# Three wide products moved between the q and k groups of a mixer, and one convolution tap moved to ScalarE

## The chip, the cores and the metric

The kernel runs on one core of one Trainium2 chip. The metric is the device time of one execution in microseconds, smaller is better. Before the change it is 1267.02 us, the median of three runs (1266.68 to 1269.48).

## What is computed

A trunk of two layers over 256 tokens of 1024 channels, in float32. Each layer is a SwiGLU, a mixer and a SwiGLU again. The mixer multiplies the normed input once by `w_in` and cuts the columns into pieces for two branches:

```python
h = rmsnorm(x, norm_mix[l])
gq, gk, gv, gz, gb, ga, c_q, c_kv, k_rope, gate_logits = split_cols(h @ w_in[l])
y_a = gdn_branch(gq, gk, gv, gz, gb, ga, gdn_conv[l], ...)
y_b = mla_branch(c_q, c_kv, k_rope, cos, sin, ...)
gates = jax.nn.sigmoid(gate_logits).reshape(B, S, N_BRANCH, D)
x = x + (gates[:, :, 0] * y_a + gates[:, :, 1] * y_b) @ w_out[l]
```

The first branch is a gated delta rule in both directions: q, k and v (512 columns each) pass through a convolution of five taps along the tokens and a SiLU, the lengths of q and k are divided out, a triangular system is solved for each of four heads and each direction, and the result is normed and multiplied by silu(z). The second branch is attention of eight heads from low-rank latents.

## The kernel before

**Products.** A float32 matrix is multiplied as two float32r parts. `weights` (L111 to L127) loads a slice of a weight matrix into `raw` by the SyncE queue (L114), ScalarE rounds it to `whi` (L122), VectorE subtracts to get `wlo` (L123); `raw`, `whi` and `wlo` have three buffers each, a `whi` holds up to 1024 columns a partition. `dense_t` (L137) then runs three TensorE products per chunk of 128 input channels and per tile of 128 tokens: L133 (`xh` by `whi`), L134 (`xh` by `wlo`), L135 (`xl` by `whi`). A block of 512 columns over eight chunks has 48 such products and four pairs `whi`, `wlo`. The sums lie in the PSUM tiles `acc`, of which there are three.

**Groups of q, k, v.** `qkv_group` (L528) makes two of the twelve chunks of channels, channel-major: 48 products of 256 columns at L536 into one `acc`; the second chunk of channels takes the weights from the last to the first. VectorE multiplies by the norm into `pre` (L543) and runs the convolution: for each of the two chunks one tap at L549 and four at L551, all on VectorE, into `cv`. ScalarE does a tanh (L555), VectorE the product (L556). `pre` and `cv` have one buffer each. Groups 2 and 3 are k, 0 and 1 are q, 4 and 5 are v.

**Inversion.** `gdn_decay` (L712) makes decay tables on GpSimd (L721, L733); `gdn_la` (L736) forms the products L741 and the matrices `LA` (L745). `gdn_base` (L759) brings the 16-blocks of `LA` into place (VectorE L769, ScalarE L771, VectorE L774, L777, L778), inverts them on GpSimd in 30 small steps (L783, L785) and brings them back (VectorE L788, L790, ScalarE L793, VectorE L794). `inv0` to `inv5` build the whole inverse with many small TensorE products, the first of them at L817. `gdn_first`, `gdn_second` and `gdn_out` (L930, then VectorE L933, ScalarE L936, GpSimd L99, VectorE L947) follow, and L472 transposes the result.

**Attention.** `mla_dense` makes q, k, v of four heads (products with latents, ScalarE L603 and L607, VectorE L608, rotation on GpSimd L589 to L594), `mla_heads` transposes them (L629, copies L632 on ScalarE). A head is L642, VectorE L644, ScalarE L650, VectorE L652 and L654, transposes L659, a copy to SBUF (L664 or L666), L671.

**Order.** The calls are written out by hand at the end of `mixer` (L980 to L1053). The SyncE queue follows that order of calls. On the other engines the framework that builds the program sets the order of instructions ahead of time from these calls and its own timing; each engine then works through its list in that order and waits at the first instruction that isn't ready. The mixer runs twice.

Of the kernel before, what the change touches and what calls it, by code (L numbers as in the profile page):

```python
# [11 lines left out]
F32 = mybir.dt.float32  # L12
# [8 lines left out]
P = 128  # L21
# [16 lines left out]
def encoder_trunk(ctx: ExitStack, tc: tile.TileContext, x, positions, norm_ffn1, ffn1_w_gate, ffn1_w_up,  # L38
# [23 lines left out]
    # the tensor engine's clock rises while the first loads run  # L62
# [8 lines left out]
    # columns of gains: ffn1 (8 per layer), mix, ffn2, q latent (3), kv latent (2), gdn (1)  # L71
# [29 lines left out]
    def split(hi, lo, ps, gain=None):  # L101
        """hi + lo = gain * ps, both exact in float32r."""
        if gain is None:
            A.copy(out=hi, in_=ps)
            V.tensor_tensor(out=lo, in0=ps, in1=hi.bitcast(F32), op=ALU.subtract)
        else:
            A.activation(out=hi, in_=ps, func=AF.Copy, scale=gain)  # L107
            V.scalar_tensor_tensor(out=lo, in0=ps, scalar=gain, in1=hi.bitcast(F32), op0=ALU.mult,  # L108
                                   op1=ALU.subtract)

    def weights(src, nk, w, pool=wpool):  # L111
        """A [nk*128, w] slice of weights, as (hi, lo) tiles of up to 1024 elements a partition."""
# [16 lines left out]
    def mm3(ps, a, w, n, start, stop, ts=range(NT)):  # L129
        """ps[t] (+)= a^T w in three passes, for the token tiles ts."""  # L130
        for t in ts:
            a1, a2 = (v[:, t * P:(t + 1) * P] for v in a)
            T.matmul(ps[t][:, :n], lhsT=a1, rhs=w[0], start=start, stop=False)  # L133
            T.matmul(ps[t][:, :n], lhsT=a1, rhs=w[1], start=False, stop=False)  # L134
            T.matmul(ps[t][:, :n], lhsT=a2, rhs=w[0], start=False, stop=stop)  # L135

    def dense_t(acts, src, c0, w, evac, tail=4, pool=wpool):  # L137
        """evac(t, psum [128 tokens, w]) of acts @ src[:, c0:c0+w]; acts: (hi, lo) [128, tokens] of each chunk.
        The last chunks (tail or fewer) go through for one token tile, then for the other."""
# [22 lines left out]
    def dense_halves(acts, parts):  # L162
        """dense_t for two parts (src, c0, evac) of 512 columns: the first half of the chunks for both, then the second."""
# [11 lines left out]
    def to_chan(srcs, hi, lo, kc, gain0=None):  # L175
        """Transposes srcs[t] ([128 tokens, n*128]) into chunks kc.. of hi / lo [128, chunk, tokens]."""
# [22 lines left out]
    def x_done(t, cg):  # L199
        """Half cg of x's tile t is final: sum of squares."""  # L200
        A.activation(out=junk, in_=x_sb[:, t, cg * 512:(cg + 1) * 512], func=AF.Square,
                     accum_out=state["ss"][:, t, cg:cg + 1])
# [67 lines left out]
    def finale(down):  # L270
        """The last x, its norm, the result; x of the first half lies by its gains before the second is there."""
# [37 lines left out]
    def mixer_consts(tmp):  # L309
# [16 lines left out]
        alog = const.tile([P, depth, 8], F32, name="alog")  # -exp(A_log)  # L326
# [12 lines left out]
        # m[p, f]  # L339
# [6 lines left out]
        # half[:, 0]: partition % 32 < 16, half[:, 1]: the others  # L346
# [7 lines left out]
        # the off-diagonal 16-blocks of the 32-blocks on the diagonal: below it (mlo) and above it (mup)  # L354
# [11 lines left out]
        # rotary tables  # L366
# [42 lines left out]
    def mixer(l, next_gain):  # L409
# [7 lines left out]
        with tc.tile_pool(name="mix", bufs=1) as mp:  # L417
# [16 lines left out]
            def rstd_row():  # L434
                """rstd along the free axis, the same in every partition."""
# [26 lines left out]
            def to_chan2(srcs, gains):  # L462
                """Chunks of 128 channels, two to a tile: a list of (hi, lo) [128, tokens]."""
# [35 lines left out]
            def gdn_scalars():  # L499
# [4 lines left out]
                # softplus(a) = max(a, 0) + log1p(exp(-|a|))  # L504
# [14 lines left out]
            qkT = mp.tile([P, 8, S], F32, name="qkT")  # L519
            vT = {}  # lies in ysb until ysb is written  # L520
# [4 lines left out]
            def qkv_group(grp):  # L525
                """Two of the twelve chunks of channels."""
# [3 lines left out]
                # one group of sums after the other: they share a bank. The second takes the weights from the last on  # L530
# [13 lines left out]
                for c in range(2):  # L544
                    ch = grp * 2 + c
                    for d in range(5):
                        wc = ccol[:, l * 60 + d * 12 + ch:l * 60 + d * 12 + ch + 1]
                        if d == 0:
                            V.tensor_scalar(out=cv[:, c], in0=pre[:, c, 0:S], scalar1=wc, scalar2=None, op0=ALU.mult)  # L549
# [3 lines left out]
                # 2 silu(.); the lengths and |k| v below take account of the 2  # L553
# [5 lines left out]
            def lengths(c0):  # L559
                """1/|.| of four of the eight heads of q and k, a column for each head."""  # L560
                pss = gdp()[:, :4 * NT * 32].rearrange("p (c t s) -> p c t s", c=4, t=NT)
                for c in (0, 2):
# [3 lines left out]
                    for g in range(4):  # L566
                        # the sums for the tokens of group g, in each of its partitions
# [28 lines left out]
            def mla_dense(hf):  # L596
                """q, k, v of four heads, token-major, rotary parts turned."""
# [22 lines left out]
            def mla_heads(q, k, v):  # L620
                """attend(pair of heads), of the four that q, k, v hold."""
# [57 lines left out]
            LA, Z, egc, cs = {}, {}, {}, {}  # L679
            LAd = {}  # L680
            for d in range(2):
                LAd[d] = mp.tile([P, NT, NH, 2, P], F32, name=f"LA{d}")  # [.., 0, :] for q, [.., 1, :] for k
# [7 lines left out]
            def gdn_coeffs():  # L690
# [3 lines left out]
                # -beta / |k|^2  # L694
# [17 lines left out]
            def gdn_decay(t):  # L712
                """E[j, h, i]: decay from token j to token i of the tile, 0 where i comes before j."""
                for d in range(2):
# [10 lines left out]
                    if t == d:  # L725
                        # first tile of this direction: decay of each token up to the carried state
# [5 lines left out]
                    # hi_m[p, f] holds where f is at or after p in this direction  # L732
# [25 lines left out]
            def gdn_base():  # L758
                """XC, ZC: inverses (and transposes) of the 16-blocks on the diagonal, each block in a partition of its  # L759
                own meanwhile."""  # L760
# [47 lines left out]
            def inv_zero():  # L808
                """Z = X^T = (1 + L)^-T from the inverted 16-blocks: blocks of 32, 64, 128 in turn."""
                for d in range(2):  # L810
                    G.memset(Z[d], 0.0)
# [21 lines left out]
            def inv2(d):  # L833
# [9 lines left out]
                # the 64-block that the last step takes X from  # L843
# [41 lines left out]
            def gdn_first(d):  # L885
                """First tile of direction d: its solution, and what it adds to the other tile."""
# [39 lines left out]
            def gdn_out(t):  # L926
# [10 lines left out]
                # o here is -|q| sqrt(128) times the true one, zs_t is 2 silu(z) / rstd  # L937
# [43 lines left out]
            rstd_row()  # L981
            qkv_group(2)
            dense(xh, xl, NKC, wl_, C_BA, 400, ev_ba)
            qkv_group(3)
            qkv_group(0)
            dense(xh, xl, NKC, wl_, C_KV, 288, ev_kv)
            gdn_scalars()
            gdn_decay(0)
            lengths(4)
            cqT = latent(cq, QL, 0, G_Q + 3 * l)  # L990
            qkv_group(1)
            gdn_decay(1)
            ckT = latent(ckv, KVL, 2, G_KV + 2 * l)
            nk_ = gdn_coeffs()
# [5 lines left out]
            dense(xh, xl, NKC, wl_, C_Z, 512, ev_z)  # L1000
# [7 lines left out]
            gb = [gate(C_G + D)]  # L1008
            gb.append(gate(C_G + D + 512))
# [46 lines left out]
    new_norm()  # L1056
    state["squares"] = False  # of the input: once its products run
# [32 lines left out]
```

## Time and profile before

| What | Value |
| --- | --- |
| median of three runs | 1267.02 us |
| span of the profiled execution, first to last instruction | 1260.2 us |
| TensorE (PE) busy | 1230.4 us, 98% |
| VectorE (DVE) busy | 774.1 us, 61% |
| ScalarE (ACT) busy | 623.4 us, 49% |
| GpSimd (POOL) busy | 132.5 us, 11% |
| mean granted TensorE clock | 0.993 |

The profile gives the profiled execution by its span; the runs' times are taken from outside, and their median is 6.8 us above the span, which is what lies ahead of the first instruction and behind the last. The kernel is a queue of TensorE work with few gaps, so it is read by looking for the stretches in which TensorE is idle or runs at a lower clock, and for what ended each wait.

### The profile page before, as it was taken

Reading aid. Unit: us, or ns where it says so; the run is one execution under the profiler, and the core shown is the slowest. Engines: PE = TensorE matmul, PEld = TensorE weight load, DVE = VectorE, ACT = ScalarE, POOL = GpSimd, SP = SyncE. Lnnn points to the kernel's source line nnn. Section 1 sums busy time; section 2 is a strip of 40 time slices with the busy share of each in tenths; the row PEclk is TensorE's granted clock in tenths of the full one; section 3 lists DMA queues with packets and bytes.
Section 4 is the critical chain, followed back from the end, with each engine's and each line's share of the span. In section 5 each row is a group of like instructions: output and inputs, shape, how many; then the busy total and the mean of one; then the engine's idle time right before and its main releaser. Section 6 shows DMA issues by size and latency. Waiting matters only on the chain.

```text
span 1260.2 us, 17612 instructions
## 1 busy us (share of the span) xinstructions
PE 1230.4 (98%) x7064; PEld 1031.9 (82%) x7064; DVE 774.1 (61%) x1127; ACT 623.4 (49%) x911; POOL 132.5 (11%) x237
## 2 busy tenths in 40 slices
PE   9999999899999999999999999998999999999997
PEld 6888889777988788888888888897778787888886
DVE  5655556986757665554555554588876576555554
ACT  6554445546445455443445443465555455544443
POOL 1000001445001000000000000015540000000010
PEclk9999999999999999999999999999999999999999
DMA  7554554435222555555555555543442245565552
GB/s 266 175 197 153 198 184 157 153 119 167 71 99 95 164 176 181 187 169 198 182 187 182 185 167 201 177 147 123 150 162 74 68 134 184 168 199 179 188 184 84
DMA packets 114576, 202.70 MB, mean 161 GB/s; under 512 B 4107, under 2 KB 30399, under 8 KB 114495
## 3 DMA queue, kind: packets, MB, share of 16 engines
q1 hardware_dynamic: 114031, 200.52, 47.8%
q8 instruction: 55, 0.90, 0.3%
q10 hardware_dynamic: 464, 1.06, 0.2%
q14 instruction: 26, 0.21, 0.1%
HBM read 200.52 MB, written 1.05 MB: 160 GB/s over the span
## 4 chain that ended last, share of the span: by engine, by line
PE 88%; DVE 4%; POOL 4%; issue 1%; ACT 1%; DMA 0%; POOLq 0%; SPq 0%; ACTq 0%
PE acc L133 24%; PE acc L134 23%; PE acc L135 23%; PE acc L536 4%; PE ms L183 2%; DVE wlo L123 2%; POOL bt L783 1%; PE ms L671 1%; PE ms L642 1%; POOL t L785 1%; PE gd L134 1%; PE gd L135 1%; PE gd L133 1%; PE gd L912 1%; DVE cv L551 1%
## 5 line engine op out<-in xcount | busy, mean ns | idle before, releaser
L123 DVE TENSOR_TENSOR wlo<-raw,whi 128x1024 fp32r<-128x1024 f32 (+3 forms) x388 | 471.2, 1217 | 371.0 <-ACT whi L122 369.0
L122 ACT CAST whi<-raw 128x1024 fp32r<-128x1024 f32 (+3 forms) x388 | 398.8, 1031 | 435.9 <-PE acc L135 392.0
L134 PE MATMUL acc<-wlo,xh 128*128 128x512 f32 (+3 forms) x968 | 360.7, 374 | 0.0
L135 PE MATMUL acc<-whi,xl 128*128 128x512 f32 (+3 forms) x968 | 357.5, 372 | 0.0
L133 PE MATMUL acc<-whi,xh 128*128 128x512 f32 (+3 forms) x968 | 344.9, 376 | 0.1
L134 PEld LDWEIGHTS acc<-wlo,xh 128*128 128x128 f32 x968 | 182.4, 188 | 29.8 <-issue 0.4
L133 PEld LDWEIGHTS acc<-whi,xh 128*128 128x128 f32 x968 | 181.4, 188 | 30.4 <-ACT xh L107 0.8
L135 PEld LDWEIGHTS acc<-whi,xl 128*128 128x128 f32 x968 | 182.1, 188 | 29.3
L134 PE MATMUL acc<-wlo,hh 128*128 128x512 f32 x352 | 138.9, 395 | 0.0
L135 PE MATMUL acc<-whi,hl 128*128 128x512 f32 x352 | 138.7, 394 | 0.0
L133 PE MATMUL acc<-whi,hh 128*128 128x512 f32 x352 | 129.1, 397 | 0.0
L135 PEld LDWEIGHTS acc<-whi,hl 128*128 128x128 f32 x352 | 65.9, 187 | 16.1
L133 PEld LDWEIGHTS acc<-whi,hh 128*128 128x128 f32 x352 | 65.9, 187 | 15.9
L134 PEld LDWEIGHTS acc<-wlo,hh 128*128 128x128 f32 x352 | 65.9, 187 | 15.3
L133 PE MATMUL acc<-whi,fr 128*128 128x512 f32 (+1 forms) x152 | 60.9, 407 | 9.2 <-DVE pre L543 7.9
L134 PE MATMUL acc<-wlo,fr 128*128 128x512 f32 (+1 forms) x152 | 61.0, 404 | 0.0
L135 PE MATMUL acc<-whi,fr 128*128 128x512 f32 (+1 forms) x152 | 58.2, 400 | 2.3 <-DVE fr L108 2.3
L536 PE MATMUL acc<-xl,whi 128*128 128x256 f32 x192 | 55.6, 289 | 0.0
L536 PE MATMUL acc<-xh,whi 128*128 128x256 f32 x192 | 55.5, 291 | 0.0
L536 PE MATMUL acc<-xh,wlo 128*128 128x256 f32 x192 | 53.3, 288 | 0.0
L551 DVE SCALAR_TENSOR_TENSOR cv<-pre,ccol,cv 128x256 f32<-128x256 f32 x96 | 51.6, 569 | 0.0
L246 ACT ACTIVATE sil<-acc,rstd 128x512 f32<-128x512 f32 (+1 forms) x48 | 31.0, 654 | 29.5 <-PE acc L135 29.4
(298 smaller groups left out, 1273.3 us busy)
## 6 DMA issues: line engine op xcount, KB each, us to landing
raw<-in_ffn_w_up_dram SPq DMA_DIRECT2D x40, 1024.0 KB, 4.9
raw<-in_ffn_w_down_dram SPq DMA_DIRECT2D x40, 1024.0 KB, 4.9
raw<-in_ffn_w_gate_dram SPq DMA_DIRECT2D x38, 1024.0 KB, 4.9
raw<-in_w_in_dram SPq DMA_DIRECT2D x32, 1024.0 KB, 4.8
raw<-in_w_out_dram SPq DMA_DIRECT2D x8, 1024.0 KB, 4.8
raw<-in_ffn_w_gate_dram SPq DMA_DIRECT2D x12, 512.0 KB, 3.5
raw<-in_ffn_w_up_dram SPq DMA_DIRECT2D x8, 512.0 KB, 3.5
raw<-in_ffn_w_down_dram SPq DMA_DIRECT2D x8, 512.0 KB, 3.3
```

What stands on the lines that cost most here:

```text
L122: A.copy(out=hi[:, :n * w], in_=raw[:, k0 * w:(k0 + n) * w])
L123: V.tensor_tensor(out=lo[:, :n * w], in0=raw[:, k0 * w:(k0 + n) * w], in1=hi[:, :n * w].bitcast(F32), op=ALU.subtract)
L133: T.matmul(ps[t][:, :n], lhsT=a1, rhs=w[0], start=start, stop=False)
L134: T.matmul(ps[t][:, :n], lhsT=a1, rhs=w[1], start=False, stop=False)
L135: T.matmul(ps[t][:, :n], lhsT=a2, rhs=w[0], start=False, stop=stop)
L183: T.transpose(out=pt[:, i * S + t * P:i * S + (t + 1) * P], in_=srcs[t][:, (j + i) * P:(j + i + 1) * P], identity=ident)
L246: A.activation(out=sil[t][:, :w], in_=ps, func=AF.Silu, scale=rstds[0][:, t:t + 1])
L536: T.matmul(pc[:, c], lhsT=w[:, cc], rhs=a, start=(i == 0), stop=(i == len(terms) - 1))
L551: V.scalar_tensor_tensor(out=cv[:, c], in0=pre[:, c, d:d + S], scalar=wc, in1=cv[:, c], op0=ALU.mult, op1=ALU.add)
L642: T.matmul(sc[:, t * S:(t + 1) * S], lhsT=qT[:, t * P:(t + 1) * P], rhs=kT, start=True, stop=True)
L671: T.matmul(po[r:r + MV, :S], lhsT=v[:, kk, h, :], rhs=prT[:, kk, :], start=(kk == 0), stop=(kk == NT - 1))
L783: G.tensor_tensor(out=tv, in0=M[:, b + 1:16, b:b + 1].to_broadcast([P, na, nb]), in1=Y[:, b:b + 1, 0:nb].to_broadcast([P, na, nb]), op=ALU ...
```

## The change

Three blocks of 512 columns are called earlier, and nothing is removed. The two gate blocks of the second branch (`gb`) move from behind `mla_dense(1)` to between the groups: the first behind group 3, the second behind `lengths(4)`. The `kv` block moves ahead of group 0. The z block moves from behind `gdn_base` to behind the second latent. In the convolution the first tap of each chunk of channels (L549) becomes a ScalarE activation that copies with a scale. Comments and docstrings are blanked, so that line numbers below L979 stay.

```diff
@@ qkv_group @@
                         if d == 0:
-                            V.tensor_scalar(out=cv[:, c], in0=pre[:, c, 0:S], scalar1=wc, scalar2=None, op0=ALU.mult)
+                            A.activation(out=cv[:, c], in_=pre[:, c, 0:S], func=AF.Copy, scale=wc)
                         else:
...
@@ order of calls @@
             rstd_row()
+
             qkv_group(2)
             dense(xh, xl, NKC, wl_, C_BA, 400, ev_ba)
             qkv_group(3)
+            gb = [gate(C_G + D)]
+            dense(xh, xl, NKC, wl_, C_KV, 288, ev_kv)
             qkv_group(0)
-            dense(xh, xl, NKC, wl_, C_KV, 288, ev_kv)
             gdn_scalars()
             gdn_decay(0)
             lengths(4)
+            gb.append(gate(C_G + D + 512))
             cqT = latent(cq, QL, 0, G_Q + 3 * l)
             qkv_group(1)
             gdn_decay(1)
             ckT = latent(ckv, KVL, 2, G_KV + 2 * l)
+            dense(xh, xl, NKC, wl_, C_Z, 512, ev_z)
             nk_ = gdn_coeffs()
...
             gdn_base()
-            dense(xh, xl, NKC, wl_, C_Z, 512, ev_z)
             inv_zero()
...
             m1 = mla_dense(1)
-            gb = [gate(C_G + D)]
-            gb.append(gate(C_G + D + 512))
             inv3(0)
```

The first place is the SyncE queue in the first part of the mixer, from group 3 on. A load of 8x256 is a q, k or v group, 4x288 the kv block, 4x512 half of a gate or z block, and `mla_w_ukv`, `mla_w_uq` are for `mla_dense`. Before:

```order
L114 DMA raw_1832<-in_w_in_dram 128x8x256
L114 DMA raw_1909<-in_w_in_dram 128x8x256
L114 DMA raw_1987<-in_w_in_dram 128x4x288
L114 DMA raw_2021<-in_w_in_dram 128x4x288
L114 DMA raw_2143<-in_w_in_dram 128x8x256
L114 DMA raw_2299<-in_mla_w_ukv_dram 128x2x512
L114 DMA raw_2323<-in_mla_w_uq_dram 128x3x384
L114 DMA raw_2477<-in_w_in_dram 128x4x512
L114 DMA raw_2511<-in_w_in_dram 128x4x512
L114 DMA raw_2730<-in_mla_w_ukv_dram 128x2x512
L114 DMA raw_2754<-in_mla_w_uq_dram 128x3x384
L114 DMA raw_2796<-in_w_in_dram 128x4x512
```

After the change:

```order
L114 DMA raw_1832<-in_w_in_dram 128x8x256
L114 DMA raw_1912<-in_w_in_dram 128x4x512
L114 DMA raw_1946<-in_w_in_dram 128x4x512
L114 DMA raw_1984<-in_w_in_dram 128x4x288
L114 DMA raw_2018<-in_w_in_dram 128x4x288
L114 DMA raw_2057<-in_w_in_dram 128x8x256
L114 DMA raw_2197<-in_w_in_dram 128x4x512
L114 DMA raw_2231<-in_w_in_dram 128x4x512
L114 DMA raw_2291<-in_w_in_dram 128x8x256
L114 DMA raw_2409<-in_w_in_dram 128x4x512
L114 DMA raw_2443<-in_w_in_dram 128x4x512
L114 DMA raw_2523<-in_mla_w_ukv_dram 128x2x512
```

Groups 3, 0 and 1 stood next to each other but for the kv block; now a block of 512 columns stands behind each of them.

The second place is ScalarE where `gdn_base` begins; `LA0` and `tb` are the matrices of the two directions, `qk` the transposed q and k of the first four heads, `m3` and `whi_3147` belong to the second four heads and to the second half of the weights of group 4. Before, from the first copy at L771 on:

```order
L771 COPY g2_2397<-LA0_1657 32x8x2x16 x4
L650 ACTIVATE pr_2974,sm_2975<-ms_2968,mxs_2971 128x256 x2
L771 COPY g2_2397<-tb_2402 32x8x2x16
L122 CAST whi_2836<-raw_2830 128x1024
L122 CAST whi_2872<-raw_2870 128x1024
L771 COPY g2_2397<-tb_2405 32x8x2x16
L122 CAST whi_2876<-raw_2870 128x1024
L771 COPY g2_2397<-tb_2408 32x8x2x16
L963 ACTIVATE gate_2792<-acc_2794,hrstd_1632 128x512
L771 COPY g2_2397<-tb_2411 32x8x2x16
```

After:

```order
L771 COPY g2_2621<-tb_2626 32x8x2x16
L632 COPY qk_2596<-ms_2591 96x512
L632 COPY qk_2603<-ms_2598 96x512
L771 COPY g2_2621<-tb_2629 32x8x2x16
L632 COPY qk_2610<-ms_2605 96x512
L607 ACTIVATE m3_2874<-acc_2876,lrs_1643 128x4x64
L607 ACTIVATE m3_2874<-acc_2877,lrs_1643 128x4x64
L632 COPY qk_2617<-ms_2612 96x512
L603 ACTIVATE m3_2873<-acc_2900,lrs_1643 128x384
L771 COPY g2_2621<-tb_2632 32x8x2x16
L771 COPY g2_2621<-tb_2635 32x8x2x16
L122 CAST whi_3147<-raw_3141 128x1024
```

Casts of gate weights stood between the copies; now it is the copies and evacuations of attention, and the next cast stands behind the last copy.

The third place is TensorE at the end of the delta rule; `gd_3673` and `gd_3701` are its outputs for token tiles 0 and 1, `ms_3602` and `ms_3585` belong to the last head of attention. Before, the last products of L930 and what follows:

```order
L930 MATMUL gd_3701<-LA1_1661 128x128
L930 MATMUL gd_3701<-LA0_1657 128x128
L930 MATMUL gd_3701<-LA1_1661 128x128
L134 MATMUL acc_3731<-wlo_3770,xh_98 128x512
L135 MATMUL acc_3731<-whi_3769,xl_99 128x512
```

After:

```order
L671 MATMUL ms_3585<-pr_3583,mv_2875 64x256 x2
L642 MATMUL ms_3588<-qk_3342,qk_3335 128x256 x2
L930 MATMUL gd_3701<-LA1_1661 128x128
L930 MATMUL gd_3701<-LA0_1657 128x128
L930 MATMUL gd_3701<-LA1_1661 128x128
L659 MATMUL ms_3602<-ident_86,pr_3594 128x128
L472 MATMUL ms_3805<-ident_86,g2_3665 128x128
L659 MATMUL ms_3602<-ident_86,pr_3594 128x128 x3
L671 MATMUL ms_3585<-pr_3607,mv_2875 64x256 x2
L472 MATMUL ms_3814<-ident_86,g2_3665 128x128
```

Behind L930 stood 22 products of a gate block and twelve of 512 columns; now the last head of attention is there, and the transposes of the result stand next to it.

## Rows read from the trace of the kernel before

**Rows 1.** Busy time by stretch: first three of mixer one, then of mixer two.

```profile
core 0: us, PE busy (x) PEld busy (x) DVE busy (x) ACT busy (x) POOL busy (x), PEclk, DMA share, GB/s
198.30:282.10 83.80, 76.07 (x479) 69.40 (x478) 72.20 (x141) 46.27 (x81) 33.21 (x43) 0.96 0.44 142
282.10:317.70 35.60, 34.18 (x179) 28.12 (x179) 26.05 (x44) 24.02 (x40) 18.05 (x39) 1.00 0.45 148
317.70:395.30 77.60, 77.22 (x852) 65.80 (x851) 48.97 (x101) 35.01 (x71) 6.15 (x10) 0.98 0.22 73
822.10:903.90 81.80, 73.96 (x475) 67.42 (x474) 71.10 (x138) 46.25 (x81) 33.32 (x43) 0.98 0.44 144
903.90:940.40 36.50, 35.08 (x185) 28.90 (x184) 27.00 (x47) 24.04 (x40) 18.06 (x39) 1.00 0.46 148
940.40:1016.70 76.30, 75.93 (x851) 64.59 (x852) 48.95 (x101) 35.21 (x72) 6.13 (x10) 1.00 0.23 75
```

**Rows 2.** The same columns, for four short windows of mixer one.

```profile
232.00:252.00 20.00, 13.80 (x83) 12.02 (x82) 19.88 (x28) 9.61 (x21) 14.38 (x13) 0.91 0.44 152
252.00:256.00 4.00, 4.00 (x21) 3.65 (x20) 0.36 (x1) 1.64 (x3) 0.00 (x0) 0.59 0.00 0
312.00:316.00 4.00, 2.58 (x23) 2.41 (x22) 3.76 (x8) 1.48 (x3) 1.15 (x3) 1.00 0.00 0
324.00:332.00 8.00, 8.00 (x182) 7.74 (x180) 4.57 (x13) 2.15 (x7) 1.19 (x4) 0.79 0.01 2
```

**Rows 3.** What TensorE waited for: total us, times, longest.

```profile
PE acc L133 <- DVE pre L543: 7.9, 2, 3.9
```

**Rows 4.** VectorE in order of time: start us, us.

```profile
235.44 2.01 DVE L549 TENSOR_SCALAR cv<-pre,ccol 128x256 f32<-128x256 f32 x2
237.53 1.90 DVE L123 TENSOR_TENSOR wlo<-raw,whi 128x1024 fp32r<-128x1024 f32 x1
...
284.49 1.21 DVE L123 TENSOR_TENSOR wlo<-raw,whi 128x1024 fp32r<-128x1024 f32 x1
```

**Rows 5.** Two scalings of 128x256, tap and ScalarE: minimum, median, maximum in ns.

```profile
L549 DVE TENSOR_SCALAR cv<-pre,ccol x24: 342/347/1127, 209.6 to 958.9; 128x256 f32<-128x256 f32 x24
L107 ACT ACTIVATE xh<-ms,gcol x48: 454/474/502, 8.3 to 1072.5; 128x256 fp32r<-128x256 f32 x48
```

**Rows 6.** TensorE in order of time (two), and from the chain (one).

```profile
287.39 0.39 PE L135 MATMUL acc<-whi,xl 128*128 128x512 f32 x1
287.61 0.39 PE L133 MATMUL acc<-whi,xh 128*128 128x512 f32 x1
...
203.85 3.83 PE acc L536 x32
```

**Rows 7.** From LA to L817, each engine's own timeline, with its wait in brackets.

```profile
283.70 0.86 DVE L745 SCALAR_TENSOR_TENSOR LA<-gd,negc,g 128x256 f32<-128x256 f32 x2
284.84 2.70 ACT L771 COPY g<-LA 32x256 f32<-32x256 f32 x4
295.44 0.65 ACT L771 COPY g<-tb 32x256 f32<-32x256 f32 x1 [1.08 <-DVE tb L769]
297.89 1.19 POOL L783 TENSOR_TENSOR bt<-t,t 128x15 f32<-128x15 f32 x1 [8.67 <-DVE t L778]
312.17 1.18 DVE L788 TENSOR_SCALAR g<-t,half 128x256 f32<-128x256 f32 x2 [4.50 <-POOL t L785]
317.63 1.91 PE L817 MATMUL gd<-XC,LA 32*32 32x32 f32 x64
```

**Rows 8.** Copies of attention on ScalarE: minimum, median, maximum in ns.

```profile
L632 ACT COPY qk<-ms x16: 567/585/597, 273.2 to 969.5; 96x512 f32<-96x512 f32 x16
```

**Rows 9.** Around L930: TensorE, VectorE and TensorE in order of time.

```profile
383.41 1.08 PE L671 MATMUL ms<-pr,mv 128*64 128x256 f32 x4
392.03 3.51 PE L930 MATMUL gd<-LA 128*128 128x128 f32 x30
393.99 0.68 DVE L933 TENSOR_TENSOR g<-gd,g 128x512 f32<-128x512 f32 x1
398.72 1.14 DVE L947 SCALAR_TENSOR_TENSOR g<-g,fac,zsil 128x128 f32<-128x128 f32 x4
403.18 0.38 PE L472 MATMUL ms<-ident,g 128*128 128x128 f32 x2
```

## The prediction

> **What bounds the kernel now.** I read busy time by stretch first, because TensorE is 98% busy over the whole span and only its gaps can be won. I cut each mixer where its chain of work changes hands: stretch 1 from the first q, k product to the last L741, stretch 2 from there to the first L817, stretch 3 from there to the last L930, stretch 4 the rest. [rows 1] show them as span, then busy time: TensorE is idle 7.7 us of stretch 1 in mixer one (83.80 less 76.07) and 7.8 us in mixer two, 1.4 us of stretch 2 in both, 0.4 us of stretch 3 in both. The granted clock shows a second loss: 0.96 and 0.98 in stretch 1, 0.98 in stretch 3 of mixer one. The two levels are 1.2 and 2.4 GHz, so a mean below 1 is time at the lower one.
>
> Second, short windows of stretch 1 [rows 2]: from 232 to 252 us TensorE is busy 13.80 of 20 us while VectorE is busy 19.88. VectorE is the limit there, not TensorE. Right behind the hole the clock is 0.59 for 4 us. Third, the waits: the longest single one of TensorE is for `pre` at L543, 3.9 us in each mixer [rows 3]: the `acc` of group 1 is held until VectorE has evacuated it, and VectorE is still at the taps of group 0, since `pre` and `cv` have one buffer. Fourth, VectorE's timeline there [rows 4]: two first taps take 2.01 us and a subtraction 1.90 us, where one elsewhere takes 1.21; GpSimd is busy 14.38 us of the same window [rows 2], and I take that as the cause of the slowness.
>
> So in stretch 1 four groups ask VectorE for more than TensorE asks of itself, bunched. In stretches 2 and 3 it is the opposite: long serial chains of small steps (inversion, attention) that wide blocks cover.
>
> **The change part by part.** A block of 512 columns costs TensorE 48 products of 0.22 to 0.23 us (the distance of two starts [rows 6]), 11 us, and VectorE four subtractions of 1.21 [rows 4], 4.9 us. A group costs TensorE 48 times 0.12 us (3.83 us for 32 [rows 6]), 5.8 us.
>
> *Stretch 1.* It gains two gate blocks, 22 us of TensorE. The z block was in it before already. The second four heads of `mla_dense` and the transposes L629 and L642 leave it for stretch 2, 8.1 us. TensorE's work is 76.1 less some 2.8 us lost to the clock, plus 22 less 8.1: 87 us. VectorE's load is 72.2 us [rows 1], plus 9.8 for the gates, less 3.3 that leaves with the heads, less the first taps: eight at 0.35 us by the median, at 1.1 us the slowest [rows 5]; I take 0.52, 4.2 us. That makes 74.5 of 87 us, 86%, the same share as before, but now each group's taps have 11 us of TensorE work beside them. The `acc` of a group is needed again only by the second block behind it. Hence the wait of [rows 3] goes. What is late next are `wlo` of the gate blocks, which stand between taps, with three buffers. I take 1.5 us of idle time for each mixer; bounds 0.5 (nothing late) and 4 (half of the present hole). Gain: 15.6 less 3.0 us idle in both mixers, and the clock: (1 less 0.96) of 83.8 is 3.4, of which some 0.9 fell into the hole and cost nothing, and 1.6 in mixer two, 4.2 together. **Stretch 1: 16.8 us faster** over both mixers.
>
> *The tap on ScalarE.* ScalarE is busy 46 of 84 us in stretch 1 [rows 1]; a scaling of 128x256 with a factor per partition takes 0.47 us there [rows 5]. VectorE's second tap must wait for it, and it stands in ScalarE's list among casts. The orders put a `wlo` between `pre` and the second tap on VectorE, which covers it: nothing. If that cover fails, it is the third rival. The Trainium skill (ScalarE: Activation LUTs, Rules for kernel authors) speaks against this move: multiplications belong on VectorE, not ScalarE. The median row agrees on the price, 0.35 against 0.47 us, but the slowest tap of the case took 1.1 us on VectorE. By the rule, 24 taps would add 24 times 0.13, 3 us, if ScalarE were on the path, and the sum would be that much later.
>
> *DMA.* SyncE's queue asks for the same loads in another order. Stretch 1 gets some 3 MB more in 88 us, 34 GB/s on 142 [rows 1], a DMA share of 0.55 instead of 0.44. One load is asked for ahead of an 11 us block: nothing.
>
> *Stretch 2.* Wide cover before it were gate blocks; now it is the second heads, groups 4 and 5 and the gate block of the first branch. Before, from the last `LA` (284.6) to the last copy L771 (296.1) it took 11.5 us [rows 7], GpSimd's steps ended at 312.2, and TensorE idled 1.4 us until then [rows 2]. Now count from the end of the last L741. TensorE has products of the second heads (2.8 + 1.6), transposes 2.1, L642 1.0, products 1.6, and half of the first pass of group 4, 12 times 0.12: 10.6 us. Then it needs the second half of group 4's weights, and that cast stands behind the last L771 in ScalarE's list. `LA` is ready at about 3. The list from there: L771 four times 2.7, a cast 1.0, eight copies L771 and L632 at 0.6 each [rows 7, 8], L607 twice and L603 1.4, cast 1.0, with no waits 11, and 14 with the transposes that two of the copies wait for. The subtraction is done 1 us later. That is a hole of 2 to 4.7 us; I take 3.9, near the upper end, since [rows 7] show L771 waiting for VectorE. Behind it 0.5 us at group 5 (its weights reuse buffers of group 4) and 0.6 at the gate block, whose third `wlo` stands behind L788, which waits for GpSimd. 5.0 us for each mixer instead of 1.4. Bounds 3 and 7. **Stretch 2: 7.2 us slower.**
>
> *Stretch 3.* It loses the cover of some 66 products of groups 4 and 5 and a gate block, 19 us; two directions of the inversion and five heads are left to cover each other. Walking the list with these durations I find TensorE waiting 1.2 us, bounds 0.5 and 3. **1.6 us slower.**
>
> *Stretch 4.* Before, from the end of L930 for tile 0 to the end of L947 it took 5.9 us (393.9 to 399.9 [rows 9]), hidden by 34 wide products, until L472 at 403.2. Now TensorE has only L930 for tile 1 (half of 3.51), one L671 (1.08) and one L642 (1.0) there: 3.8 us. Next in its list is L659 of the last head, whose input VectorE normalizes only after L947: 5.9 + 0.9. It waits 3.0 us. Then come 0.8 us for the copy before L671 and 0.4 before the projection of the last heads: 4.3 us. Bounds 2 (L642 later than I count) and 5. **8.6 us slower.**
>
> *Clock.* Four holes of 1.4 us and more are new. Of the four present ones of that size outside the big ones (two in each mixer), one was followed by a drop, at 324 to 332 us, worth 0.21 of 8, 1.7 us [rows 2]. Four more holes: one such drop, **1.7 us slower**; bounds 0 and one behind every second hole at the big hole's 2.6, 5.2.
>
> Sum: 16.8 - 7.2 - 1.6 - 8.6 - 1.7 = -2.3, that is 2.3 us slower. On the span of 1260.2 this makes 1262.5, and with the 6.8 us that lie around it, 1269.3. The profiled span and the median belong to each other within the runs' scatter, so I add the sum to the median.
>
> **The rivals.**
> - *Even trade (forecast):* 1269.3, chance 0.42. Its own range is 1264 to 1274.
> - *The late holes are half as large.* For it: the walk above counts each wait at its full length, and in the present stretches 2 and 3 TensorE hardly waits. Against: the third place of the order leaves no wide product to slip in. Holes of 2.5 and 2.15 us, no drop of the clock: 16.8 - 2.2 - 1.6 - 4.3 = 8.7, 1258.3. With all lower bounds 1256. Chance 0.33.
> - *The inversion becomes the bound.* `LA` comes some 4 us later, because VectorE has two blocks more ahead of it, and all of that lands in stretch 2, as nothing wide is left behind it: 9 us of hole, and the clock falls after it in both mixers, 5.2 us. 16.8 - 15.2 - 1.6 - 8.6 - 5.2 = -13.8, 1280.8. It decides once the last `LA` comes more than 7 us behind the last L741 (now 2.5). Against: VectorE's share in stretch 1 doesn't rise. Chance 0.17.
> - *The taps don't relieve VectorE,* since they wait behind casts of 1.05 us on ScalarE. Half of the first hole stays, 3.9 instead of 1.5: 4.8 us, 1274.1. Chance 0.08.
>
> **How the numbers follow.** A difference of 0.2% (2.5 us) is about what a measurement of this kernel can tell from no change. Of the even trade a half lies within it, a tenth below, the rest above; the second case is nearly all faster, the last two nearly all slower. Faster 0.36, same 0.24, slower 0.40. The range runs from all lower bounds of the second case to the third, 1256 to 1280, and leaves out its tails.
>
> **What would show it.** Right: TensorE idle under 2 us and the clock 1.00 in stretch 1 (no wait for `pre`); a new wait of 2 to 5 us in group 4, for `whi` or `wlo`; a wait of about 3 us before L659 of the last head, behind L947. Wrong: no wait between L930 and L472, or more than 4 us of idle time left in stretch 1.

## The result and the profile after

The changed kernel takes 1286.16 us (median of four runs, 1280.85 to 1289.42), the kernel before beside it 1266.85 us (1260.67 to 1269.48). The ratio is 1.0163 with a 95% interval of 1.0127 to 1.0198: 1.6% slower, outside the range of 1256 to 1280. In the profiled executions the span goes from 1260.2 to 1287.7 us, 27.5 us more, and the mean granted clock from 0.993 to 0.977. The profiled execution of the changed kernel is the slowest of its four, and that of the kernel before is among the faster ones, so they differ by more than the medians, 19.3 us. (In the four runs of the changed kernel the time is 1.7 us above the span. So the 6.8 us which the section on the time before puts down to what lies around the span are for the most part a difference between executions.)

First the view of [rows 1] for the changed kernel: busy time by stretch, the four stretches of mixer one, then of mixer two (stretch 4 up to the last L472).

```profile
core 0: us, PE busy (x) PEld busy (x) DVE busy (x) ACT busy (x) POOL busy (x), PEclk, DMA share, GB/s
198.30:285.90 87.60, 86.54 (x530) 78.18 (x529) 72.64 (x134) 55.51 (x93) 30.22 (x37) 1.00 0.52 160
285.90:325.90 40.00, 35.56 (x212) 30.45 (x210) 30.46 (x56) 25.88 (x45) 20.39 (x47) 1.00 0.47 152
325.90:395.40 69.50, 66.31 (x739) 54.34 (x737) 32.74 (x76) 24.51 (x65) 6.51 (x9) 0.83 0.11 36
395.40:441.10 45.70, 41.06 (x175) 31.94 (x176) 29.43 (x49) 20.02 (x33) 1.09 (x2) 0.93 0.35 116
835.60:923.30 87.70, 86.66 (x530) 78.23 (x530) 72.79 (x134) 55.50 (x93) 30.22 (x37) 1.00 0.51 159
923.30:963.40 40.10, 35.64 (x213) 30.46 (x212) 30.57 (x56) 25.97 (x45) 20.39 (x47) 1.00 0.47 150
963.40:1030.90 67.50, 64.95 (x738) 53.63 (x737) 32.83 (x76) 24.52 (x64) 6.51 (x9) 0.85 0.11 37
1030.90:1076.20 45.30, 40.91 (x175) 31.82 (x176) 29.33 (x49) 20.04 (x33) 1.09 (x2) 0.92 0.36 117
```

Two numbers are read from each row: the idle time of TensorE (span less PE busy) and the clock lost, that is, the time that the lower clock cost ((1 less PEclk) times span). Over both mixers, before and after:

| Stretch | idle before | idle after | clock lost before | clock lost after |
| --- | --- | --- | --- | --- |
| 1 | 15.6 | 2.1 | 5.0 | 0 |
| 2 | 2.8 | 8.9 | 0 | 0 |
| 3 | 0.7 | 5.7 | 1.6 | 21.9 |
| 4 | 1.3 | 9.0 | 0 | 6.8 |
| sum | 20.4 | 25.7 | 6.6 | 28.7 |

5.3 us more idle time and 22.1 us more at the lower clock make 27.4 of the 27.5 us. So in these two executions four fifths of the loss are clock, and most of that lies in stretch 3.

The hole of stretch 1 [rows 2] is gone. The same 20 us of mixer one in the changed kernel:

```profile
232.00:252.00 20.00, 20.00 (x134) 18.57 (x133) 15.59 (x18) 13.40 (x24) 12.59 (x10) 1.00 0.67 211
```

Now stretch 3 of mixer one in windows of 4 us, the same columns:

```profile
322.00:326.00 4.00, 4.00 (x21) 3.13 (x20) 4.00 (x10) 3.99 (x7) 0.00 (x0) 1.00 0.66 205
326.00:330.00 4.00, 4.00 (x125) 3.63 (x125) 4.00 (x8) 2.34 (x4) 0.00 (x0) 1.00 0.44 107
330.00:334.00 4.00, 4.00 (x80) 3.54 (x77) 3.60 (x8) 0.90 (x4) 1.76 (x3) 0.55 0.56 216
334.00:338.00 4.00, 4.00 (x77) 3.24 (x76) 1.35 (x5) 2.01 (x6) 0.00 (x0) 0.50 0.02 4
338.00:342.00 4.00, 4.00 (x34) 3.33 (x32) 1.87 (x5) 0.80 (x2) 0.79 (x2) 0.50 0.00 0
342.00:346.00 4.00, 4.00 (x86) 3.24 (x85) 0.44 (x2) 0.36 (x1) 0.00 (x0) 0.74 0.02 4
```

TensorE is busy 4.00 of 4.00 us in every row, and yet the clock goes to its lower level for 14 us. What it did there, TensorE in order of time (start, duration):

```profile
325.95 1.91 PE L817 MATMUL gd<-XC,LA 32*32 32x32 f32 x64
...
328.48 1.81 PE L825 MATMUL gd<-t,ZC 32*32 32x32 f32 x61
...
330.23 2.76 PE L817 MATMUL gd<-XC,LA 32*32 32x32 f32 x61
332.92 1.97 PE L671 MATMUL ms<-pr,mv 128*64 128x256 f32 x4
...
336.33 2.88 PE L825 MATMUL gd<-t,ZC 32*32 32x32 f32 x61
339.14 0.80 PE L133 MATMUL acc<-whi,fr 128*128 128x512 f32 x1
```

Between 326 and 339 us there is no wide product, only blocks of 32 columns and a few steps of attention. 61 records of L817 take 2.76 us where 64 took 1.91 (the trace has two records for each of these products, and can miss some), and the first wide product takes 0.80 instead of 0.39 [rows 6]. The ends of such records are modelled: one of L817 lasts 0.19 us in the trace, though the next starts 0.03 us later. So 4.00 of 4.00 says that TensorE waited for nothing, not that it was full. The last waits TensorE had before the fall lie at 318 to 320 us, with 5 us of wide products behind them and a clock of 1.00.

The longest waits of TensorE (total, times, longest); the wait of [rows 3] is no longer among them:

```profile
PE ms L659 <- DVE pr L654: 6.1, 2, 3.2
PE acc L134 <- DVE wlo L123: 4.2, 5, 1.4
PE acc L133 <- DVE mv L608: 3.0, 2, 1.5
```

### The profile page after: what moved, and what is told of

It reads as the page before. It is cut to its first block, busy times and chain, and to the rows that moved or that the text cites. A ratio compares the mean times of both kernels' runs of the same rounds, so it can differ in the third digit from the quotient of the medians.

```text
span 1287.7 us, 17613 instructions
## 1 busy us (share of the span) xinstructions
PE 1252.4 (97%) x7064; PEld 1045.5 (81%) x7064; DVE 763.9 (59%) x1103; ACT 632.2 (49%) x935; POOL 129.9 (10%) x237
## 4 chain that ended last, share of the span: by engine, by line
PE 89%; DVE 4%; POOL 3%; ACT 2%; issue 1%; DMA 0%; SPq 0%; POOLq 0%; ACTq 0%; DVEq 0%
PE acc L133 24%; PE acc L134 24%; PE acc L135 24%; PE acc L536 3%; PE ms L183 2%; PE ms L671 1%; DVE wlo L123 1%; POOL bt L783 1%; PE ms L642 1%; DVE cv L551 1%; ACT whi L122 1%; PE gd L134 1%; PE gd L135 1%; PE gd L133 1%; POOL t L785 1%
## 5 line engine op out<-in xcount | busy, mean ns | idle before, releaser
L123 DVE TENSOR_TENSOR wlo<-raw,whi 128x1024 fp32r<-128x1024 f32 (+3 forms) x388 | 465.9, 1203 | 386.8 <-ACT whi L122 385.2
```

The costliest lines, as they stand in the source:

```text
L123: V.tensor_tensor(out=lo[:, :n * w], in0=raw[:, k0 * w:(k0 + n) * w], in1=hi[:, :n * w].bitcast(F32), op=ALU.subtract)
```

## The experiments

Three readings were set against each other. Theory 1: the clock falls where narrow products (32 and 64 columns) run with little wide work between them, and the blocks that left stretch 3 were that wide work. Theory 2 blames the tap on ScalarE. Theory 3, the prediction's own: the clock falls behind waits.

A help for reading all runs: each run's time multiplied by its own mean clock. For the kernel before, 62 runs beside the first three groups of experiments took between 1259.0 and 1269.9 us at clocks of 0.995 to 0.984, and the product is 1249 to 1253 us in all of them. So most of its scatter of 11 us is clock, and the product (called the time at full clock below) separates waits and work from clock. It is 1259 us for the changed kernel: over all its runs some 7 of the 19 us lost are waits and work, and the rest is clock. The table sums up; the counts are from the order of the built programs, for one mixer, between the first L817 and the first L896 (two numbers where the mixers differ): wide products of 512 columns (behind a plus the products of q, k, v groups, of 256 columns, where there are any), and the longest row of other products, steps of attention among them, with none of these between.

| Kernel | ratio to before (95%) | clock of its runs | time at full clock, median | wide | longest narrow row |
| --- | --- | --- | --- | --- | --- |
| before | 1 | 0.984 to 0.995 | 1252 | 67+48 | 64 |
| changed | 1.0163 (1.0127 to 1.0198) | 0.975 to 0.983 | 1259 | 12, 18 | 148, 192 |
| a_tap_vector | 1.0074 (1.0045 to 1.0104) | 0.977 to 0.990 | 1254 | 18 | 166, 178 |
| b_tap_scalar | 0.9968 (0.9945 to 0.9991) | 0.984 to 0.991 | 1245 | 72+38 | 64 |
| b_gates | 1.0172 (1.0123 to 1.0221) | 0.973 to 0.974 | 1251 | 14, 8 | 206, 246 |
| a_gate2_late | 0.9925 (0.9896 to 0.9953) | 0.983 to 0.997 | 1242 | 23 | 114 |
| b_gate1_early | 0.9898 (0.9850 to 0.9947) | 0.991 to 0.998 | 1244 | 34 | 72 |
| one_gate_later | 1.0027 (1.0003 to 1.0051) | 0.992 to 0.996 | 1259 | 58 | 68 |

**The parts.** The tap alone, in both directions:

```diff
-A.activation(out=cv[:, c], in_=pre[:, c, 0:S], func=AF.Copy, scale=wc)
+V.tensor_scalar(out=cv[:, c], in0=pre[:, c, 0:S], scalar1=wc, scalar2=None, op0=ALU.mult)
```

> The changed kernel with the first tap back on VectorE. Theory 1 (the clock falls where products of 32 and 64 columns run with few wide ones between them): the moved blocks stay moved, the granted clock stays 0.975 to 0.985, the time 1.0% to 2.0% above the kernel before. Theory 2 (the tap on ScalarE delays casts, and the late waits come from there): the time comes back to within 0.4% of the kernel before, with the clock above 0.988.

> The kernel before with only the first tap moved to ScalarE. Theory 1: some 60 wide products and 38 of 256 columns stay between the first L817 and the last L930, so the clock stays above 0.99; TensorE's idle time in stretch 1 falls from 7.7 to 4 to 6 us in each mixer; 0.2% to 0.6% faster than the kernel before. Theory 2: slower than the kernel before by more than 0.3%, with new waits of TensorE behind casts.

Without the tap's move the changed kernel is 0.74% above the kernel before instead of 1.63%: neither theory's number, since a good half of the loss is gone and the rest stays. Its time at full clock is 5 us lower and its clock higher, so the tap on ScalarE costs both, with the gates moved. In the kernel before the same move wins 0.3%, as theory 1 had it: stretch 1 idles 1.8 instead of 7.7 us (78.70 less 76.87 below). But theory 1 expected a clock above 0.99 with that many wide products left, and the runs show 0.984 to 0.991. Both mixers have the same order of instructions there, and in this execution one lost 8 us of clock in stretch 3 and the other none:

```profile
198.20:276.90 78.70, 76.87 (x496) 69.80 (x495) 68.20 (x135) 53.50 (x97) 35.90 (x47) 1.00 0.48 151
310.60:392.00 81.40, 80.45 (x828) 67.13 (x828) 45.91 (x96) 35.60 (x79) 6.22 (x10) 0.90 0.21 66
934.60:1007.70 73.10, 72.29 (x828) 60.91 (x828) 46.88 (x96) 34.12 (x73) 6.48 (x10) 1.00 0.23 73
```

**The gates.** The kernel before with both gate blocks moved, and with the first alone:

```diff
             qkv_group(3)
+            gb = [gate(C_G + D)]
             qkv_group(0)
...
             lengths(4)
+            gb.append(gate(C_G + D + 512))
...
```

> The kernel before with both gate blocks moved, and z, kv and the taps as they were. 20 wide products are left between the first L817 and the last L930. Theory 1: the clock lost in stretch 3 is as in the changed kernel, 8 to 13 us in each mixer, the clock 0.975 to 0.985; 1.0% to 2.0% slower than the kernel before: the gates alone make the loss. Rival (z, kv or the taps make it): within 0.4% of the kernel before.

> The kernel before with one of the two gate blocks moved between groups 3 and 0, nothing else. By the order 44 wide products are left between the first L817 and the last L930, where the kernel before has 84 and 48 of 256 columns, and the changed kernel 22. Theory 1: the clock lost in stretch 3 lies between the two, 3 to 8 us in each mixer; stretch 1 idles under 3 us; between 0.4% faster and 0.8% slower than the kernel before. Theory 3 (the clock falls behind waits of 1.4 us and more, as the prediction had it): no more such waits than in the kernel before, so no more clock lost than there, and 0.5% or more faster.

Both gates alone make the whole loss, 1.7%; z, kv and the taps aren't needed for it. The time at full clock is that of the kernel before, 1251 us, so all of this loss is clock. Stretches 2 and 3 in mixer two:

```profile
922.60:966.70 44.10, 37.82 (x206) 31.70 (x205) 36.72 (x70) 24.92 (x42) 18.96 (x41) 0.93 0.45 144
966.70:1031.60 64.90, 63.21 (x723) 53.92 (x723) 25.88 (x65) 21.78 (x57) 5.70 (x8) 0.78 0.05 18
```

Stretch 3 idles 1.7 us and loses 14.3 to the clock: the kernel with the fewest wide products there has the lowest clock. Another 3 us go in stretch 2, behind a wait of 4.5 us. One gate is the other way: 1.0% faster than before, the best kernel of all. A second measurement of it (one_gate_again) gave 0.9897 (0.9858 to 0.9937).

> The kernel with one gate block between groups 3 and 0 once more, for a narrower interval and the scatter of its clock. 0.7% to 1.3% faster than the kernel before; the runs differ by their clock (0.990 to 0.998) and time multiplied by clock is the same for all within 0.2%, 1243 to 1246 us.

Stretches 1 to 3 of mixer one there, then stretch 3 of mixer two:

```profile
198.20:283.40 85.20, 84.30 (x530) 76.22 (x528) 73.27 (x142) 52.36 (x88) 33.68 (x43) 1.00 0.51 161
283.40:323.40 40.00, 38.21 (x214) 31.29 (x213) 33.85 (x61) 24.01 (x41) 18.28 (x41) 1.00 0.44 139
323.40:384.50 61.10, 60.20 (x752) 50.05 (x752) 36.12 (x81) 26.30 (x62) 7.06 (x8) 0.97 0.16 53
...
939.70:999.20 59.50, 58.60 (x752) 49.08 (x752) 36.20 (x81) 26.32 (x62) 7.05 (x8) 1.00 0.16 54
```

It idles 0.9 us in stretch 1, about as the changed kernel does, 1.8 in stretch 2 and 0.9 in stretch 3, and loses 1.8 us of clock in one mixer and none in the other (5.1 and none in the first measurement). Here theory 1 missed and theory 3 had it right, that the kernel gains over 0.5%: with 34 wide products left the clock costs less than the 3 to 8 us a mixer that theory 1 gave. The changed kernel with only its second gate block put back agrees:

> The changed kernel with the second gate block back behind the second heads, everything else as changed. 23 wide products between the first L817 and the first L896 and a longest unbroken row of narrow ones of 114, where the changed kernel has 12 to 18 and 148 to 192. Theory 1: stretch 2 idles under 2.5 us instead of 4.4, the clock lost in stretch 3 is 4 to 9 us a mixer instead of 10 to 12; 0.8% to 2% faster than the changed kernel, between 0.8% faster and 0.6% slower than the kernel before. Rival (the second block isn't what matters): 1.2% to 2% slower than the kernel before.

It is 0.75% faster than the kernel before, within theory 1's range, and 2.3% faster than the changed one (0.9925 by 1.0163), a little more than that theory gave; stretch 2 does not idle at all, and the clock loses 1.8 and 8.6 us in its two stretches 3. So the second gate block, beside the first, is the part that turns a gain into a loss. Stretch 2 of mixer one and stretch 3 of both:

```profile
284.90:323.40 38.50, 38.50 (x217) 32.52 (x215) 32.23 (x58) 26.54 (x46) 18.25 (x41) 1.00 0.51 164
323.40:383.70 60.30, 58.80 (x745) 48.28 (x745) 33.30 (x77) 25.87 (x66) 6.12 (x8) 0.97 0.11 37
938.70:1004.90 66.20, 64.70 (x745) 52.76 (x745) 33.39 (x77) 26.14 (x66) 6.12 (x8) 0.87 0.10 35
```

**The place and the tap.** One block between groups 0 and 1 instead (its call behind `lengths(4)`), without and with the tap on ScalarE; and the tap's move beside the block in the first place:

> One gate block where the change puts the second one, between groups 0 and 1. By the order 58 wide products are left between the first L817 and the first L896 (34 with the block between groups 3 and 0), and the longest unbroken row of narrow products is 68 (72). Theory 1: the clock stays at or above that of the other place, lost 0 to 5 us a mixer; the wait for pre is gone, stretch 1 idles 1 to 4 us; 0.4% to 1.3% faster than the kernel before. Rival: the hole moves to the next groups, stretch 1 idles over 5 us and nothing is won (within 0.3% of the kernel before).

> The same and the first tap on ScalarE. 48 wide products are left there and the longest unbroken row of narrow ones is the same 68, where the tap's move made it 178 with the block in the other place. Theory 1: so the tap's move costs no clock here, and relieves VectorE: within 0.3% of the same kernel without it, or up to 0.4% faster. Rival (the tap on ScalarE by itself costs time once the hole is gone): 0.4% to 0.9% slower than without it, as it was in the other place.

> One gate block between the groups (the best kernel so far) and the first tap on ScalarE. By the order 27 wide products are left between the first L817 and the last L930, where without the tap's move there are 44. Theory 1: the idle time stays under 10 us, but 3 to 10 us more clock is lost than with one gate alone (5.1): 0.2% to 0.8% slower than that one. Rival (the tap only relieves VectorE): the same or faster.

Here theory 1 missed. The clock was as high as expected (0.992 to 0.996), but the hole came back: stretch 1 of mixer one idles 6.8 us, of which one wait takes 3.5. The stretch in the columns of [rows 1]:

```profile
198.00:285.70 87.70, 80.90 (x504) 72.94 (x503) 73.90 (x141) 49.55 (x83) 36.34 (x43) 0.98 0.47 148
```

Its longest wait, of two:

```profile
PE acc L134 <- DVE wlo L123: 7.1, 2, 3.5
```

The taps of group 0 still stand ahead of the subtraction that the block's second weights need. With the tap on ScalarE that stretch idles 2.9 us and the kernel is 0.82% faster than before (0.9918, 0.9887 to 0.9949), more than theory 1 expected from the tap. In the first place, where no hole is left, the same move costs: 0.9963 (0.9931 to 0.9996) against 0.9898. Its time at full clock is even lower, 1238 against 1244 us, but the clock of its runs falls to 0.975 to 0.990: the longest narrow row goes from 72 to 178 and 184. That is theory 1's price, 0.65%.

**Added work.** The direct trial: products that do nothing, put into the changed kernel ahead of each of the twelve steps of the inversion in a mixer. They are of bfloat16 and use all 128 rows and columns of the array, where the kernel's own narrow ones are float32 blocks of 32 by 32.

```diff
+            def wide():
+                ps = gdp()
+                for _ in range(2):
+                    T.matmul(ps[:, :512], lhsT=junk[:, :P], rhs=junk[:, :512], start=True, stop=True)
+                return ps
...
-                pv = blocks(gdp(), 0, 32)
+                pv = blocks(wide(), 0, 32)
```

> The changed kernel with work added that does nothing: two products of 512 columns ahead of each step of the inversion, 48 in all, 0.22 us each at the full clock, 10.6 us; 20 of the 24 of a mixer stand between the first L817 and the last L896. Theory 1 (narrow products without wide ones let the clock fall): the clock lost falls from 29 us to under 15, and the kernel is between 10 us faster and 2 us slower than the changed one, in spite of the work. Theory 3 (waits let it fall): the waits stay, the clock lost stays 25 to 30 us, and the kernel is 8 to 12 us slower than the changed one.

> The control: at the same places 16 products of 32 columns instead of two of 512, the same number of columns, more instructions. Theory 1 if what counts is that the products are wide: the clock lost in stretch 3 stays over 20 us in both mixers, and the kernel is 5 to 25 us slower than the changed one. If any added work would do (TensorE kept from waiting): the clock lost falls under 15 as with the wide ones.

> The changed kernel with one product of 512 columns that does nothing ahead of each step of the inversion, 24 in all, 5.3 us. The earlier control (16 products of 32 columns) had as many columns as this, and half of those of two wide ones, other than its expectation said. By the order the rest stands nearly as in the changed kernel, and the longest unbroken row of narrow products falls from 148 and 192 to 66. If wide products hold the clock: lost in stretch 3 between 3 and 15 us over both mixers (21.9 in the changed kernel, 24.3 with the narrow control), and 0 to 1% faster than the changed kernel in spite of the work. If only the number of added columns counts: as much clock lost as with 16 narrow ones, 20 us and more, and 3 to 6 us slower than the changed kernel.

> The control with as many columns as two wide products: 32 products of 32 columns at each step. If the width of the products counts: clock lost in stretch 3 still 15 to 30 us over both mixers. If the added columns count, however they are cut: 4.8 us or less, as with two wide ones.

Stretch 3 of both mixers with two wide ones, 16 narrow ones, one wide one and 32 narrow ones, in this order:

```profile
324.70:393.70 69.00, 65.70 (x757) 51.88 (x763) 33.49 (x78) 25.46 (x66) 7.47 (x9) 0.93 0.12 42
959.00:1023.30 64.30, 61.69 (x757) 49.06 (x763) 33.54 (x78) 25.45 (x66) 7.53 (x9) 1.00 0.14 45
```

```profile
325.30:395.40 70.10, 68.70 (x900) 58.44 (x900) 32.99 (x78) 24.86 (x66) 5.60 (x8) 0.85 0.11 36
958.00:1030.80 72.80, 71.40 (x900) 61.05 (x900) 33.03 (x78) 24.96 (x66) 5.59 (x8) 0.81 0.11 35
```

```profile
325.70:395.50 69.80, 67.50 (x748) 54.12 (x747) 33.00 (x76) 24.59 (x65) 6.51 (x9) 0.85 0.11 36
963.20:1031.50 68.30, 66.00 (x748) 53.02 (x747) 32.97 (x76) 24.49 (x65) 6.48 (x9) 0.88 0.11 37
```

```profile
326.30:396.10 69.80, 68.48 (x1059) 58.61 (x1059) 32.35 (x78) 24.97 (x65) 5.64 (x8) 0.93 0.11 36
958.70:1029.30 70.60, 69.28 (x1059) 59.61 (x1059) 32.39 (x78) 25.00 (x65) 5.64 (x8) 0.90 0.10 35
```

| Added per step | idle in stretch 3 | clock lost there | ratio to before (95%) | clock of its runs | lost in a whole run, median |
| --- | --- | --- | --- | --- | --- |
| nothing (changed) | 5.7 | 21.9 | 1.0163 (1.0127 to 1.0198) | 0.975 to 0.983 | 26 |
| two of 512 | 5.9 | 4.8 | 1.0185 (1.0144 to 1.0225) | 0.981 to 0.990 | 19 |
| 16 of 32 | 2.8 | 24.3 | 1.0159 (1.0119 to 1.0199) | 0.978 to 0.981 | 26 |
| one of 512 | 4.6 | 18.7 | 1.0223 (1.0189 to 1.0258) | 0.977 to 0.979 | 28 |
| 32 of 32 | 2.6 | 12.0 | 1.0161 (1.0130 to 1.0193) | 0.984 to 0.989 | 15 |

The columns on stretch 3 are of one execution each; the last is (1 less the mean clock) times span over the four runs of each kernel, other stretches included. The profiled execution with two wide ones is the best of its four, at 0.990, so its 4.8 us are probably less than that kernel mostly loses there.

Theory 3 falls: with 16 narrow ones half of the waits are gone and as much clock is lost as without, and with two wide ones the waits are as before and clock comes back, 17 of 22 us in the profiled execution and some 8 of 26 in the median. Theory 1 is right that the loss hangs on what TensorE is given to do in this stretch, but not in its word "wide". One wide product, with as many columns as 16 narrow ones, missed its expectation: over its runs it holds the clock no better than they do, and the kernel is slower, not faster. 32 narrow ones, with as many columns as two wide ones, came out between the two readings in stretch 3, 12.0 us, and over all runs they lose no more than the two wide ones. That points to the number of columns added, however they are cut; that their width counts too is not shown. The rest of the order shifts a little in each kernel, so the figures are no finer than that. Nor do these trials tell whether narrow blocks of the kernel's own kind, 32 by 32 in float32, would have done the same. A busy share of 1.00 tells nothing of it.

No filler pays. Two wide ones cost 10 us at full clock (1269.6 against 1259.4) for what they give back, and come out 0.2% above the changed kernel; 16 narrow ones only fill waits (1258.8) and change nothing. With one gate moved, two wide ones ahead of six steps took 6 us at full clock (1249.9 against 1244.2), and the clock was no steadier and no higher, 0.983 to 0.997 (0.991 in the median, against 0.996 over both measurements of one gate alone); the ratio is 0.9973 (0.9944 to 1.0001), and theory 1's expectation missed:

> One gate block between the groups, with two products of 512 columns that do nothing ahead of six of the inversion's steps: 24 in all, 5.3 us, of which 8 products stand where TensorE waits or has wide work. One gate alone lost 0 us of clock in one mixer and 5.1 in the other. Theory 1: no clock lost in either, and the time within 0.3% of one gate alone, with less scatter. Theory 3: 5 us slower.

## Why the prediction was wrong

- **Stretch 1**, 16.8 us faster: right, 18.5. Idle time falls by 13.5 us (predicted 12.6) and 5.0 us of clock return (4.2). VectorE is busy 72.6 of 87.6 us, 83% (predicted 86%).
- **Stretch 2**, 7.2 us slower: right in size, 6.1, not in place. The last `LA` comes 2.1 us behind the last L741, as counted. The cast for group 4 does stand behind the last L771, but the one wait for it is only 0.3 us, since TensorE had already lost 1.5 to `mv` (L608) and 0.4 to the copies; the gate block then waits 1.4 for `wlo`.
- **Stretch 3**, 1.6 us slower: too small, 5.0 us of idle time. In mixer one it is six waits of 0.2 to 0.8 us at six places, most of them in the inversion and the delta rule.
- **Stretch 4**, 8.6 us slower: right, 7.8. The mixers wait 3.2 and 2.9 us before L659 of the last head, and each 0.7 before L671 and 0.6 before the projection; the prediction said 3.0, 0.8 and 0.4.
- **Clock**, 1.7 us slower, bounds 0 and 5.2: this step failed. It said that four new holes would bring one such drop, and counted drops by holes. Idle time in all was forecast to rise by 4.8 us and rose by 5.3; the clock was to give 2.5 us back and took 22.1. Of the 28.7 us lost in the changed kernel 21.9 lie in stretch 3, most of them where TensorE waited for nothing.
- **The tap**, nothing: wrong too. With the gates moved it costs 0.9%, about 5 us of waits and work and the rest clock (1259 against 1254, 0.9795 against 0.9865 in the median). The prediction priced it by VectorE's list alone. The rule of the Trainium skill weighed there (ScalarE: Activation LUTs, Rules for kernel authors) pointed the right way in the two kernels without a hole in stretch 1, and the wrong way in the kernel before and with the block in the later place, where the move won 0.3 and 1.1%.

The reason given for the clock was wrong, not only its size. The one drop outside the big holes, at 324 to 332 us [rows 2], stood in the row that refutes it: TensorE busy 8.00 of 8 us, with 182 records of products. It was taken as a consequence of the hole before it. In the trace of the changed kernel some 15 of the 29 us lost follow narrow products with TensorE busy throughout, 7 more narrow products with waits of up to 0.6 us among them, and only the two drops of 3.4 us in stretch 4 follow a long wait, those of 3.2 and 2.9 us. The prediction saw that stretch 3 loses 19 us of wide cover and asked only what TensorE would wait for without it. The rival nearest in time, the inversion as the bound at 1280.8 us, was not what happened: its condition, `LA` over 7 us late, was not met, and stretch 2 lost no clock.

The Trainium skill (TensorE: Matmul & The Clock Gate, HAM oscillation — how this bites in real kernels) explains falls of the clock by waits of TensorE between groups of products. Stretch 4 of mixer one agrees with that, a wait of 3.2 us and a clock of 0.52 in the 4 us behind it; stretch 3 shows a fall at 330 us with TensorE's last wait ended at 320.

What stays open is why moving z and kv beside both gates lifts the clock (b_gates against a_tap_vector, 0.973 against 0.987), other than that 18 instead of 8 to 14 wide products are left; and why one mixer drops and the other, with the same order, does not. Nor does the count of wide products order the kernels above some 30 of them: the runs' clock is 0.991 to 0.998 with 34 (b_gate1_early), 0.995 to 0.998 with 48 (one_gate_later_tap), and 0.984 to 0.991 with 72 (b_tap_scalar).

## What to carry to other kernels

Before moving wide products out of a stretch, list what is left there in the engine's order: a stretch of small products that shows 100% busy can still lose half its clock, and the moved work was paying for that. Fill a hole with the least work that closes it: one block won 1.0%, the second turned that into a loss of 1.6%. When runs of one kernel scatter, multiply each time by its clock; if the products agree, the scatter is clock, and two kernels can be compared in waits and in clock apart. The product is good to a few us only: in b_gate1_tap it falls from 1241 to 1235 us as the clock falls from 0.990 to 0.975.

## What the runs showed of the hardware

The granted clock fell with TensorE busy in every window of 4 us, during products of 32 columns, and stayed low for 14 us; executions of the kernel before differ by 11 us, mostly by their mean clock (0.984 to 0.995). Products of 32 columns added to such a stretch brought the clock back in part when there were enough of them: with 32 a step the runs' clock is 0.984 to 0.989, with 16 it is 0.978 to 0.981, without any 0.975 to 0.983. Moving a scaling of 128x256 from VectorE (0.35 us [rows 5]) to ScalarE (0.50 us in the changed kernel) won 0.3 and 1.1% where VectorE held TensorE, and cost 0.65 and 0.9% where no such hole was left.
